# Loading and turning the FFN convolution's weights later in a one-core hybrid decoder layer

## The chip, the cores and the metric

The kernel runs on one core of a Trainium2 chip. The metric is the device time of one execution in microseconds; a median of several runs is given. A profile of one execution shows every instruction on the engines: PE (matmul) with PEld (its weight loads), DVE (vector), ACT (scalar), POOL (GpSimd), and SP, whose queue issues most of the DMAs. "L261" is line 261 of the kernel file, and names such as `raw` or `mT` are the program's tiles.

## The reference

One layer of a decoder for a prompt of 1024 tokens and 8 single-token samples, all in float32. Condition vectors `c` give shift, scale and gate of two modulations; then come a gated delta rule and sliding-window attention side by side, and an FFN with a short causal convolution on its gate. Cut to what matters here:

```python
sh1, sc1, gt1, sh2, sc2, gt2 = split(silu(c) @ w_mod + b_mod, 6)
h = rmsnorm(x, norm1_w) * (1 + sc1) + sh1
qkv, gdn_gate, beta, a, sq, sk, sv, ga, gb = split(h @ w_in)
y_a = gdn_out(delta_rule(silu(conv4(qkv, gdn_conv_w)), beta, a), gdn_gate) @ w_gdn_out
y_b = window_attention(sq, sk, sv, swa_sinks) @ w_swa_out
x = x + gt1 * ((sigmoid(ga) * y_a + sigmoid(gb) * y_b) @ w_o)
h2 = rmsnorm(x, norm2_w) * (1 + sc2) + sh2
gc = causal_dwconv3(h2 @ w_ffn_gate, ffn_conv_w) + ffn_conv_b
x = x + gt2 * ((silu(gc) * (h2 @ w_ffn_up)) @ w_ffn_down)
y = rmsnorm(x, final_norm_w)
```

`ffn_conv_w` (3 x 2816) and `ffn_conv_b` (2816) are the two inputs that the change is about. They are first needed in the FFN, in the last third of the program.

## The kernel before

Every float32 product is made of three matmuls on operands that are split into a high and a low part (`mm3`, L178 to L182; the split is L129 on ACT and L130 on DVE). Activations are kept turned, with channels on the 128 partitions, in three parts of the tokens: 384, 384 and 264 (the last with the 8 samples). Each part is normed by rows (L287 to L290: a square with a sum on ACT, a power on POOL, a scaling on DVE), turned by PE transposes (L190), modulated (L326 on ACT, L328 on DVE) and split into `b1h` and `b1l`.

The change lies in the head of the program, the first 60 us or so:

- `conditioning` (L220 on) loads `c`, applies silu and turns it into `cTr`.
- `vectors` (L192 to L218) gathers the small vectors as rows of a tile, one row for each run of 128 channels, and turns them with PE transposes, so that each becomes a column per channel tile. Biases of the modulation, the norms' weights and the delta rule's convolution are loaded on ACT's queue into `pc`. The FFN convolution's weights (66 rows of 128) and bias (22 rows) are loaded on SP's queue (L204, L205) into a tile `pp`. There are three transposes into one bank `pt`, and then copies on DVE: `vecs`, `cw`, and `fcw`, the FFN convolution's weights and bias times a half (L218).
- `modulation(lo)` makes four channel tiles of the modulation: four loads of 512 KB of `w_mod` into `qst` (L261), sixteen matmuls of 128x512 into the bank `sc` (L264), a copy `mrows` (L267), four small matmuls (L270, two instructions each in the trace), and the addition of the bias into `mT` (L271). It runs for the tiles 8, 0, 12 and 4, in this order.
- Between them stand the loads and norms of the first 384 tokens (three tiles of 128 rows: `raw`, `raw`, `V`), the modulation of channel tiles 0 to 3 as soon as the first two calls are done and of 4 to 7 after the last two, and the early weights: four loads of `w_in` (512 KB each, L135), each split into a high and a low part (`wh`/`wl`, `wmh`/`wml`, `obt`).

Who comes first on an engine is not set by the order of this code. The kernel is built with a scheduler that orders the instructions of each engine and each queue by its own estimate of when they are ready; `issue_after(x)` only forbids an instruction to stand ahead of `x`. Small edits can so move instructions far away. On each engine the instructions then run in order. DMAs report through eight semaphores that are used in turn, so that a DMA also waits for the one that had its semaphore before.

After the head, attention runs with projections of the delta rule as filler, then the delta rule's heads, the branches' output, and the second half with the FFN. `fcw` is read there (L1571 to L1575 and L1678).

## Time and profile before

| | |
|---|---|
| median of 3 runs | 2088.38 us |
| lowest and highest run | 2085.28 us, 2094.0 us |
| span of the profiled execution, first to last instruction | 2084.4 us |
| PE busy | 2012.7 us (97%) |
| DVE, ACT, POOL busy | 1347.8, 900.2, 520.2 us |
| moved by DMA | 275.75 MB |

The profile gives no device time of its own execution besides the span; the lowest of the three runs lies 0.9 us above that span and the median 4.0 us. In the rows below, a row of the timeline has the start, the duration, the engine, the line, the operation, the tiles (output<-inputs), shapes, a count and, in brackets, how long the engine had been idle before it and what ended that. "SPq" is the time in which SP's queue issues a DMA. A row of the windows has, after the stretch, the busy time and count of PE, PEld, DVE, ACT and POOL, the granted clock of PE (1.00 is full), the mean busy share of the DMA engines and the GB/s.

### The profile page before, as it was taken

How to read it: one execution, taken by the hardware profiler on the slowest of the kernel's cores; microseconds unless marked ns; L12 is line 12 of the kernel's file. 1: busy time of each engine (PE TensorE's matmuls, PEld its weight loads, DVE VectorE, ACT ScalarE, POOL GpSimd, SP SyncE). 2: the span in 40 equal slices, each digit the busy share in tenths (PEclk: the TensorE clock that was granted, in tenths of full speed). 3: DMA queues.
4: the chain of work that ended last, by engine and by line, in shares of the span. 5: the costliest groups of instructions: out<-in, count | busy, mean ns of one | idle time of the engine just before them, and what ended most of it. 6: DMA issues, size and time to landing. Idle time of an engine off the chain costs nothing.

```text
span 2084.4 us, 41297 instructions
## 1 busy us (share of the span) xinstructions
PE 2012.7 (97%) x16245; PEld 1910.2 (92%) x16245; DVE 1347.8 (65%) x2714; ACT 900.2 (43%) x2233; POOL 520.2 (25%) x594
## 2 busy tenths in 40 slices
PE   7999998999999999989989999999999999999897
PEld 4987877799999999989989999999999999999897
DVE  5755768473655647656544675578876776767756
ACT  4664545433344243432342542354444444534443
POOL 2000000121321221201111000005575466446421
PEclk9999999999999999999999999999999999999999
DMA  8256443331332322312275855323333333488862
GB/s 300 62 144 210 135 167 116 117 94 51 80 80 61 73 72 52 89 42 62 63 223 172 285 186 163 112 63 97 105 91 112 102 92 112 136 305 266 291 215 94
DMA packets 301887, 275.75 MB, mean 132 GB/s; under 512 B 59730, under 2 KB 248111, under 8 KB 301676
## 3 DMA queue, kind: packets, MB, share of 16 engines
q1 hardware_dynamic: 295642, 252.14, 39.6%
q0 software_dynamic: 5552, 20.37, 2.8%
q8 instruction: 127, 2.08, 0.4%
q14 instruction: 68, 0.56, 0.1%
q10 hardware_dynamic: 498, 0.61, 0.1%
HBM read 212.93 MB, written 62.51 MB: 132 GB/s over the span
## 4 chain that ended last, share of the span: by engine, by line
PE 83%; DVE 5%; DMA 5%; ACT 3%; issue 1%; SPq 1%; POOL 1%; DVEq 0%; POOLq 0%; ACTq 0%
PE mm L180 19%; PE mm L181 18%; PE mm L182 18%; PE wv L180 3%; PE wv L182 3%; PE wv L181 3%; PE wy L182 2%; PE wy L180 2%; PE wy L181 2%; PE pv L652 1%; PE pt L190 1%; PE tp L190 1%; DVE x L1472 1%; PE mm L264 1%; PE rc L954 1%
## 5 line engine op out<-in xcount | busy, mean ns | idle before, releaser
L180 PE MATMUL mm<-b1h,wh 128*128 128x384 f32 (+1 forms) x1520 | 496.9, 328 | 3.7 <-ACT gt L1294 1.6
L181 PE MATMUL mm<-b1l,wh 128*128 128x384 f32 (+1 forms) x1520 | 489.3, 323 | 0.0
L182 PE MATMUL mm<-b1h,wl 128*128 128x384 f32 (+1 forms) x1520 | 488.0, 323 | 0.3 <-DVE wl L130 0.3
L180 PEld LDWEIGHTS mm<-b1h,wh 128*128 128x128 f32 x1520 | 286.7, 189 | 12.4 <-issue 4.6
L181 PEld LDWEIGHTS mm<-b1l,wh 128*128 128x128 f32 x1520 | 287.1, 189 | 4.4 <-issue 3.1
L182 PEld LDWEIGHTS mm<-b1h,wl 128*128 128x128 f32 x1520 | 286.3, 189 | 3.9 <-issue 2.8
L129 ACT ACTIVATE wh<-raw 128x1024 fp32r<-128x1024 f32 x83 | 87.0, 1049 | 122.4 <-PE mm L181 70.2
L130 DVE TENSOR_TENSOR wl<-raw,wh 128x1024 fp32r<-128x1024 f32 x82 | 101.0, 1233 | 57.2 <-ACT wh L129 55.1
L181 PE MATMUL mm<-pk,w 128*128 128x260 f32 (+1 forms) x440 | 124.8, 284 | 1.1 <-DVE pk L130 1.1
L180 PE MATMUL mm<-pk,w 128*128 128x260 f32 (+1 forms) x440 | 124.8, 284 | 0.0
L182 PE MATMUL mm<-pk,w 128*128 128x260 f32 (+1 forms) x440 | 124.5, 283 | 0.0
L130 DVE TENSOR_TENSOR w<-ws,w 128x512 fp32r<-128x512 f32 x88 | 78.0, 886 | 36.9 <-ACT w L129 36.7
L1626 ACT COPY bml<-mm 128x256 f32<-128x256 f32 (+1 forms) x132 | 48.9, 371 | 100.6 <-PE mm L182 96.7
L180 PE MATMUL mm<-bmh,w 128*128 128x260 f32 (+1 forms) x320 | 90.3, 282 | 0.0
L182 PE MATMUL mm<-bmh,w 128*128 128x260 f32 (+1 forms) x320 | 90.1, 282 | 0.0
L1681 DVE SCALAR_TENSOR_TENSOR fa<-fz,fcw,fa 128x512 f32<-128x512 f32 x88 | 75.2, 874 | 18.2 <-ACT fa L1679 17.9
L180 PE MATMUL mm<-b2h,wh 128*128 128x384 f32 (+1 forms) x256 | 83.2, 328 | 2.9 <-ACT wh L129 2.8
L181 PEld LDWEIGHTS mm<-pk,w 128*128 128x128 f32 x440 | 83.2, 189 | 1.3 <-DVE pk L130 1.3
L181 PE MATMUL mm<-b2l,wh 128*128 128x384 f32 (+1 forms) x256 | 83.6, 327 | 0.4 <-DVE b2l L130 0.4
L180 PEld LDWEIGHTS mm<-pk,w 128*128 128x128 f32 x440 | 83.2, 189 | 0.2 <-ACT bml L1626 0.2
L182 PEld LDWEIGHTS mm<-pk,w 128*128 128x128 f32 x440 | 83.4, 190 | 0.0
L182 PE MATMUL mm<-b2h,wl 128*128 128x384 f32 (+1 forms) x256 | 82.8, 326 | 0.0
(645 smaller groups left out, 5886.2 us busy)
## 6 DMA issues: line engine op xcount, KB each, us to landing
raw<-in_w_in_dram SPq DMA_DIRECT2D x59, 512.0 KB
ws<-in_w_ffn_down_dram SPq DMA_DIRECT2D x55, 256.0 KB
raw<-xd SPq DMA_DIRECT2D x47, 258.0 KB
raw<-in_w_ffn_down_dram SPq DMA_DIRECT2D x47, 256.0 KB
raw<-in_w_ffn_gate_dram SPq DMA_DIRECT2D x22, 512.0 KB
raw<-in_w_ffn_up_dram SPq DMA_DIRECT2D x22, 512.0 KB
qst<-in_w_mod_dram SPq DMA_DIRECT2D x16, 512.0 KB
raw<-in_w_mod_dram SPq DMA_DIRECT2D x16, 512.0 KB
```

What stands on the lines that cost most here:

```text
L129: self.nc.scalar.activation(hi, x, AF.Copy)
L130: (eng or self.nc.vector).tensor_tensor(lo, x, hi.bitcast(F32), op=ALU.subtract)
L180: mm(ps, whi, xhi, start=first, stop=False, **kw)
L181: mm(ps, whi, xlo, start=False, stop=False, **kw)
L182: self.last_mm = mm(ps, wlo, xhi, start=False, stop=last, **kw).ins
L190: self.nc.tensor.transpose(out, in_, self.ident[:p, :p])
L264: nc.tensor.matmul(ps[32 * j:32 * j + 32], self.cT[:, k0 + j, :], ws[j // 2][:, j % 2, :], start=k0 == 0, stop=k0 > 0)
L652: nc.tensor.matmul(pv[64 * r:64 * r + 64], V[:, n - back, ch], ps[:, r::2, :], start=back == 0, stop=back == (n > 0))
L954: yield step(nc.tensor.matmul(ds, kd[:, n, :], s, start=True, stop=True))
L1472: nc.vector.scalar_tensor_tensor(x[:, :np_], ps[:, :np_], by[:, j, 8:9], x[:, :np_], op0=ALU.mult, op1=ALU.add)
L1626: self.last_copy = nc.scalar.copy(r[p, i], x[p])
L1681: nc.vector.scalar_tensor_tensor(ai[:, c:e], zi[:, j + c:j + e], col(j), ai[:, c:e], op0=ALU.mult, op1=ALU.add)
```

## The change

The two loads, the transpose and the scaling of the FFN convolution's vectors leave `vectors` and become a function of their own with two halves, `ffn_vectors`. The first half issues the loads, not ahead of the last weight load that the code has issued, into a tile `new` (a name, and a buffer, that the decays of the delta rule use later on); it is called behind the fourth early weight. The second half turns them into a bank of `pt` of its own and writes `fcw`; it is called when the first part's modulation is written.

```diff
--- before.py
+++ after.py
@@ vectors
-        rows2 = self.t(pool, [P, P], "pp")
-        nc.sync.dma_start(rows2[0:66, :], I["ffn_conv_w"][0].rearrange("j (n p) -> (j n) p", p=P))
-        nc.sync.dma_start(rows2[66:88, :], I["ffn_conv_b"][0].rearrange("(n p) -> n p", p=P))
         ps = self.t(psum, [P, 512], "pt")
         self.transpose(ps[:, 0:65], rows[0:65, 0, :])
         self.transpose(ps[:, 128:224], rows[0:96, 1, :])
-        self.transpose(ps[:, 256:344], rows2[0:88, :])
...
+    def ffn_vectors(self, pool, psum):
+
+        nc, I = self.nc, self.I
+        rows = self.t(pool, [P, P], "new", bufs=1)
+        with self.tc.issue_after(self.w_load.ins):
+            nc.sync.dma_start(rows[0:66, :], I["ffn_conv_w"][0].rearrange("j (n p) -> (j n) p", p=P))
+            nc.sync.dma_start(rows[66:88, :], I["ffn_conv_b"][0].rearrange("(n p) -> n p", p=P))
+        yield
+        ps = self.t(psum, [P, 512], "pt")
+        self.transpose(ps[:, 0:88], rows[0:88, :])
         self.fcw = self.const([P, 4, FT], "fcw")
-        nc.vector.tensor_scalar_mul(self.fcw, ps[:, 256:344].rearrange("p (j n) -> p j n", j=4), 0.5)
+        nc.vector.tensor_scalar_mul(self.fcw, ps[:, 0:88].rearrange("p (j n) -> p j n", j=4), 0.5)
+        yield
@@ run
                 self.early.append(self.win(COL_SQ + P, tags=("obt", "obt"), home=pool))
+                ffn = self.ffn_vectors(pool, psum)
+                next(ffn)
                 self.xs[2] = self.load_rows(pool, 2, ("raw", "raw", "V"))
                 self.modulate_part(pool, psum, 0, xs, self.a1, 0, range(4, KC))
+                next(ffn)
                 self.attention(pool, psum)
```

The scheduler moves much else with it. In the changed file the lines behind `vectors` are 8 higher (L280 becomes L288), those behind the new calls 11. On SP's queue, at the program's start, the rows stood so before (`raw` and `V` from `x_prompt` are the first 384 token rows):

```order
L224 DMA qst_100<-in_c_sample_dram 8x1024
L225 DMA qst_100<-in_c_prompt_dram 1x1024
L204 DMA pp_133<-in_ffn_conv_w_dram 66x128
L205 DMA pp_133<-in_ffn_conv_b_dram 22x128
L280 DMA raw_181<-in_x_prompt_dram 128x1024
L261 DMA qst_156<-in_w_mod_dram 128x2x512
L261 DMA qst_158<-in_w_mod_dram 128x2x512
L261 DMA qst_164<-in_w_mod_dram 128x2x512
L261 DMA qst_166<-in_w_mod_dram 128x2x512
L280 DMA raw_183<-in_x_prompt_dram 128x1024
L280 DMA V_185<-in_x_prompt_dram 128x1024
L261 DMA qst_204<-in_w_mod_dram 128x2x512
```

At the same place they stand so now:

```order
L232 DMA qst_100<-in_c_sample_dram 8x1024
L233 DMA qst_100<-in_c_prompt_dram 1x1024
L288 DMA raw_175<-in_x_prompt_dram 128x1024
L288 DMA raw_177<-in_x_prompt_dram 128x1024
L288 DMA V_179<-in_x_prompt_dram 128x1024
L269 DMA qst_150<-in_w_mod_dram 128x2x512
L269 DMA qst_152<-in_w_mod_dram 128x2x512
L269 DMA qst_158<-in_w_mod_dram 128x2x512
L269 DMA qst_160<-in_w_mod_dram 128x2x512
L269 DMA qst_198<-in_w_mod_dram 128x2x512
L269 DMA qst_200<-in_w_mod_dram 128x2x512
```

The two small loads are gone from here and all three token tiles stand ahead of the first `w_mod` load; the set of large loads up to the first `w_in` load, which comes two `w_mod` loads further down in both, is the same. The small loads now stand as the 29th and 30th DMA of the queue, behind the fourth `w_in` load and ahead of the third part's token rows.

On DVE, around the second modulation (`mrows`, then `mT`), the rows stood so before (`wl` is the low part of the first early weight):

```order
L267 COPY mrows_172<-sc_155 128x512
L288 TENSOR_SCALAR ss_192<-ss_192 128x1
L271 TENSOR_TENSOR mT<-sc_174,vecs 128x36
L290 TENSOR_SCALAR raw_183<-raw_183,ss_192 128x1024
L275 SCALAR_TENSOR_TENSOR a_154<-mT,vecs 128x36
L288 TENSOR_SCALAR ss_197<-ss_197 128x1
L290 TENSOR_SCALAR V_185<-V_185,ss_197 128x1024
L267 COPY mrows_220<-sc_203 128x512
L271 TENSOR_TENSOR mT<-sc_222,vecs 128x36
L328 TENSOR_SCALAR pp_232<-pt_228,a_154,mT 128x384
L130 TENSOR_TENSOR wl_289<-raw_286,wh_288 128x1024
```

They stand so now:

```order
L298 TENSOR_SCALAR V_179<-V_179,ss_191 128x1024
L275 COPY mrows_166<-sc_149 128x512
L279 TENSOR_TENSOR mT<-sc_168,vecs 128x36
L283 SCALAR_TENSOR_TENSOR a_148<-mT,vecs 128x36
L275 COPY mrows_214<-sc_197 128x512
L130 TENSOR_TENSOR wl_283<-raw_280,wh_282 128x1024
L279 TENSOR_TENSOR mT<-sc_216,vecs 128x36
L336 TENSOR_SCALAR pp_226<-pt_222,a_148,mT 128x384
```

The scaling of the second and third token tile has moved ahead of the first modulation's end, and `wl` has moved ahead of the second modulation's `mT`. The same happens at the fourth modulation, where the second weight's `wl` stands ahead of `mT`.

On PE, behind the fourth modulation, the last transposes of the first part's tokens stood before behind two matmuls of the second early weight (`mm_593`, whose first row is the transposes' neighbour here):

```order
L180 MATMUL mm_593<-b1h_10_148,wh_319 128x384
L181 MATMUL mm_593<-b1l_11_149,wh_319 128x384
L190 MATMUL pt_364<-ident,raw_181 128x128
L190 MATMUL pt_364<-ident,raw_183 128x128
L190 MATMUL pt_364<-ident,V_185 128x128
```

Now they stand behind twelve of `mm_594`, the same product, and two of the third weight (the last five of these rows and the transposes' first):

```order
L180 MATMUL mm_594<-b1h_9_142,wh_313 128x384
L181 MATMUL mm_594<-b1l_10_143,wh_313 128x384
L182 MATMUL mm_594<-b1h_9_142,wl_314 128x384
L180 MATMUL mm_623<-b1h_9_142,wmh_319 128x384
L181 MATMUL mm_623<-b1l_10_143,wmh_319 128x384
L190 MATMUL pv_369<-ident,raw_175 128x128
```

Twelve matmuls have moved from behind the transposes to ahead of them. The transpose of the FFN vectors stands about thirty matmuls further down on PE, between two transposes of the second part's tokens; on POOL a fill of `new` for the delta rule's decays, which must wait for it, now stands ahead of the third part's three powers. Further on, PE's order differs in most rows of the attention stage, in two stretches of the delta rule and in one of the output; every engine has the same operations as before.

## The prediction

> **What bounds the kernel now.** The page first: PE is busy for nearly the whole span, and the chain that ended last is 83% PE.

> ```profile
> span 2084.4 us, 41297 instructions
> PE 2012.7 (97%) x16245; PEld 1910.2 (92%) x16245; DVE 1347.8 (65%) x2714; ACT 900.2 (43%) x2233; POOL 520.2 (25%) x594
> PE 83%; DVE 5%; DMA 5%; ACT 3%; issue 1%; SPq 1%; POOL 1%; DVEq 0%; POOLq 0%; ACTq 0%
> ```

> PE is idle for 71.7 us in all (2084.4 - 2012.7), so nothing that leaves PE's work alone can win more. The change touches the head, so I read the windows there next.

> ```profile
> 5.00:10.00 5.00, 2.94 (x15) 1.51 (x15) 2.17 (x7) 1.44 (x3) 2.85 (x8) 1.00 1.02 382
> 15.00:20.00 5.00, 3.21 (x14) 1.41 (x14) 2.53 (x7) 0.86 (x2) 1.11 (x2) 0.79 1.07 378
> 20.00:25.00 5.00, 4.04 (x24) 1.69 (x22) 0.81 (x2) 1.06 (x1) 0.00 (x0) 0.87 1.09 366
> 25.00:30.00 5.00, 4.87 (x24) 2.05 (x24) 4.37 (x8) 3.22 (x6) 0.00 (x0) 1.00 1.05 387
> 45.00:50.00 5.00, 5.00 (x33) 4.90 (x32) 3.39 (x7) 4.93 (x10) 2.51 (x3) 1.00 0.41 140
> ```

> DMA is full (share over 1.0, 366 to 387 GB/s) while PE has gaps up to 25 us; from 25 us PE is nearly full, from 40 us wholly. The head is thus a race of loads against PE's first work. Third, SP's queue in the timeline, for when the loads start, and the waits of ACT and DVE, for when they land.

> ```profile
> 1.53 0.29 SPq L204 DMA_DIRECT2D pp<-in_ffn_conv_w_dram  x1
> 1.87 0.35 SPq L205 DMA_DIRECT2D pp<-in_ffn_conv_b_dram  x1
> 2.74 0.36 SPq L280 DMA_DIRECT2D raw<-in_x_prompt_dram  x1
> 3.16 2.07 SPq L261 DMA_DIRECT2D qst<-in_w_mod_dram  x4
> 5.27 0.47 SPq L280 DMA_DIRECT2D raw<-in_x_prompt_dram  x1
> ...
> 6.25 1.06 ACT L287 ACTIVATE vch<-raw 128x1024 f32<-128x1024 f32 x1 [0.96 <-DMA raw<-in_x_prompt_dram]
> 13.44 1.06 ACT L287 ACTIVATE vch<-raw 128x1024 f32<-128x1024 f32 x1 [6.04 <-DMA raw<-in_x_prompt_dram]
> 21.90 1.06 ACT L129 ACTIVATE wh<-raw 128x1024 fp32r<-128x1024 f32 x1 [6.04 <-DMA raw<-in_w_in_dram]
> 35.55 1.06 ACT L129 ACTIVATE wh<-raw 128x1024 fp32r<-128x1024 f32 x1 [6.13 <-DMA raw<-in_w_in_dram]
> ```

> These rows give one law. Large load 1 (tokens) lands at 6.25, load 6 (the second token tile) at 13.44, load 12 (the first `w_in`) at 21.90: (21.90 - 6.25)/11 = 1.42 us a load, (13.44 - 6.25)/5 = 1.44. Loads land one behind the other, at a pace that the queue's start alone shifts. Last, the steps of the modulation on DVE and PE.

> ```profile
> 15.01 0.69 DVE L267 COPY mrows<-sc 128x512 f32<-128x512 f32 x1 [4.08 <-PE sc L264]
> 17.02 0.74 DVE L290 TENSOR_SCALAR raw<-raw,ss 128x1024 f32<-128x1024 f32 x1
> 20.88 2.11 PE L264 MATMUL sc<-qst,cTr 128*32 128x512 f32 x12
> 23.04 0.69 DVE L267 COPY mrows<-sc 128x512 f32<-128x512 f32 x1 [3.69 <-PE sc L264]
> 24.88 0.20 DVE L271 TENSOR_TENSOR mT<-sc,vecs 128x36 f32<-128x36 f32 x1 [1.15 <-PE sc L270]
> 25.13 1.05 PE L264 MATMUL sc<-qst,cTr 128*32 128x512 f32 x4 [0.29 <-DVE mT L271]
> 25.70 1.22 DVE L130 TENSOR_TENSOR wl<-raw,wh 128x1024 fp32r<-128x1024 f32 x1
> 34.31 1.92 PE L264 MATMUL sc<-qst,cTr 128*32 128x512 f32 x16 [0.29 <-DVE mT L271]
> 38.15 0.20 DVE L271 TENSOR_TENSOR mT<-sc,vecs 128x36 f32<-128x36 f32 x1 [1.15 <-PE sc L270]
> 39.12 0.44 PE L190 MATMUL pt<-ident,raw 128*128 128x128 f32 x2 [0.55 <-DVE pp L328]
> ```

> The second modulation is late although its loads are not: load 11, its last, should land at 6.25 + 10 x 1.42 = 20.5, yet PE does twelve of its matmuls in one run at 20.88 to 22.99, behind the transposes of token tiles that landed as loads 6 and 7 and were scaled from 17.02 on.

> **Part by part.** *The two loads leave the queue's head.* Token load 1 stands where the first of them stood: it is issued at 1.53 instead of 2.74, 1.21 us earlier. It has no wait for an earlier DMA now, and the third token tile is the one that waits. Every load of equal rank lands 1.21 us earlier; the 44 KB less are 0.1 us more, left out. [...]

> *Token tiles 2 and 3 move ahead of the first modulation's loads.* Load 7 is now the first modulation's last: 6.25 - 1.21 + 6 x 1.42 = 13.6. With its last four matmuls (1.05) that modulation ends near 14.7, no later than before, when its copy began at 15.01; and the norms' scalings now fall into that wait. Load 11 is still the second modulation's last: 5.04 + 14.2 = 19.2, and its last four matmuls (1.05) end near 20.3 instead of 22.99.

> *`wl` moves ahead of `mT` on DVE.* That takes some back: the first `w_in` (load 12) lands at 21.90 - 1.21 = 20.69, ACT's high part takes 1.06, DVE's low part 1.22, so `mT` comes at about 22.97 and not at 21.8. Queued behind `wl` on DVE are `mT` and the first modulated tile, and PE's third modulation waits for them. Before `mT` was at 24.88: 1.9 us gained.

> *To the fourth modulation* PE runs the same instructions without a gap (25.13 to 34.31), so the 1.9 us hold; its last load, number 20, is due at 5.04 + 19 x 1.42 = 32.0, in time. Its `mT` waits for the second `wl`: `w_in` at 35.55 - 1.21 = 34.34, plus 1.06 and 1.22, 36.6 against 38.15: 1.5 us. But PE no longer waits there. Before, it did two matmuls and stood still for 0.55 us until the transposes; now twelve more stand ahead of them. Two later rows give their pace:

> ```profile
> 40.50 0.34 PE L182 MATMUL mm<-b1h,wl 128*128 128x384 f32 x1
> 40.68 0.33 PE L180 MATMUL mm<-b1h,wh 128*128 128x384 f32 x1
> ```

> Twelve at 0.175 to 0.18 us are 2.1 us. By the steps above the transposes would end near 39.8, as they do before, with these twelve done: the head is 2.1 us ahead. I take **-2.1**, with bounds of 0 (a later wait eats it) and -3.2 (22.99 - 20.3, and the 0.55, if `wl` takes nothing back).

> *The moved operations themselves.* One transpose and one scaling:

> ```profile
> 8.37 0.35 PE L190 MATMUL pt<-ident,pp 88*128 88x88 f32 x1
> 9.07 0.24 DVE L218 TENSOR_SCALAR fcw<-pt 128x88 f32<-128x88 f32 x1
> ```

> At 8 us PE was waiting anyway; at 45 us it is full (5.00 of 5), so the transpose now costs 0.1 to 0.35. I take 0.2, the middle. Its loads go behind the fourth `w_in`, which waits for the second `wl` (36.6), and PE is there thirty matmuls behind 39.8, near 45: they have some 8 us, and if that cover were gone, PE and POOL's powers behind the fill of `new` would wait for one load, 1.4 us. DVE has 3.39 of 5 busy there, so the scaling is taken at 0, at most 0.24. The sum: -2.1 + 0.2 = **-1.9**.

> *The reshuffle behind the head.* No operation is added, but PE's order changes in the attention stage. Its gaps lie here:

> ```profile
> 340.00:350.00 10.00, 9.12 (x93) 7.63 (x91) 8.88 (x15) 4.87 (x10) 1.01 (x1) 1.00 0.44 148
> 350.00:360.00 10.00, 6.16 (x66) 4.65 (x64) 7.96 (x33) 7.98 (x37) 0.00 (x0) 1.00 0.13 52
> 360.00:370.00 10.00, 7.95 (x52) 5.68 (x52) 7.11 (x25) 6.46 (x25) 0.51 (x1) 1.00 0.10 23
> 370.00:380.00 10.00, 7.63 (x49) 5.44 (x49) 5.96 (x21) 6.09 (x27) 0.00 (x0) 1.00 0.14 55
> ```

> PE idles 0.88 + 3.84 + 2.05 + 2.37 = 9.1 us, waiting for the softmax between short runs of filler. The new order there has the same pattern (mostly six filler matmuls between the score groups, one place with none), so I take 0; the bounds are a gain of 9.1 and as much lost.

> **Sum.** The span goes from 2084.4 to 2082.5. The runs lie up to 9.6 us above the span and their median 4.0; I carry 1.9 us over to the median: 2088.38 - 1.9 = 2086.5 us. About 0.5%, 10.4 us, is what a measurement of this kernel can tell from no change (its own three runs spread over 8.7), so this counts as no change.

> **The rivals.**

> *The head's gain is eaten.* Attention's first scores wait for the softmax on DVE and ACT, and ACT is full at 45 us (4.93 of 5). If those set the pace, PE's lead of 2.1 us becomes a wait: 2088.4. For it speaks ACT's row; against it PE's, which is as full.

> *Slower: filler misplaced in attention.* Each score group there lacks cover by about a microsecond now. If the new order puts filler where PE has cover and leaves it out where it hasn't, six matmuls (1.05 us) of stall are added at each such place; to pass 10.4 us it would take twelve places, the 9.1 us more than doubled: 2086.5 + 12.6 = 2099. I see one place of this kind in the new order, which speaks against it.

> *Faster: filler covers attention.* The reverse, all 9.1 us filled and the head's 1.9: 2077.4, just past 0.5%. The same pattern speaks against it.

> *A colder PE.* The granted clock was 0.79 in the window of 15 to 20 us, where PE was busy for 3.21 of 5. With tokens ahead of `w_mod`, PE waits for the first modulation's loads until about 9 us and again between them. If that lowers the clock for as long again as in the two windows from 15 to 25 us, 5 x 0.21 + 5 x 0.13 = 1.7 us are lost and the gain is nearly gone: 2088.2. [...]

> **How the numbers follow.** The forecast (head ahead by about 2 us, the rest within 3) has 0.62; the eaten gain 0.18 and the colder PE 0.08, both no change; slower by attention 0.06; faster by attention 0.06. So 0.06 faster, 0.88 the same, 0.06 slower. The range takes the two cases of no gain, a few microseconds of reshuffle either way and the spread of a median of such runs (about 3 us): 2080 to 2094.

> **What would show it.** Right: the first token load issued near 1.5; the second modulation's copy near 20.3 and its `mT` near 23; `wl` before it; no gap of PE before the transposes at 39 us; PE's sum over the first 60 us up by about 2 us; idle between 340 and 380 us within 3 of 9.1. Wrong: loads that land at the old times, DVE waiting for `w_in` ahead of `mT` for longer than 1.2 us, PE waiting at the FFN vectors' transpose, or any stage behind 100 us that changes by more than the head.

## The result and the profile after

The changed kernel takes 2092.61 us (median of 21 runs, 2088.42 to 2101.8) against 2088.28 us for the kernel before in 21 runs beside them: ratio 1.0023, 95% interval [1.0012, 1.0034]. That is within 0.5%, as forecast, but slower by 4 to 5 us where 1.9 us were to be gained. The profiled execution has a span of 2088.8 us (before 2084.4). First its page: PE is busy 2.0 us longer with as many instructions, and its idle time has grown by 2.4 us (2088.8 - 2014.7 = 74.1 against 71.7).

```profile
span 2088.8 us, 41308 instructions
PE 2014.7 (96%) x16245; PEld 1911.1 (91%) x16245; DVE 1355.7 (65%) x2714; ACT 902.1 (43%) x2233; POOL 525.4 (25%) x594
```

**The head.** SP's queue (first rows) starts with the tokens, as forecast; ACT has the first `w_in`, and DVE the modulations' steps.

```profile
1.53 0.83 SPq L288 DMA_DIRECT2D raw<-in_x_prompt_dram  x2
2.77 0.33 SPq L288 DMA_DIRECT2D V<-in_x_prompt_dram  x1
```

```profile
21.04 1.06 ACT L129 ACTIVATE wh<-raw 128x1024 fp32r<-128x1024 f32 x1 [11.43 <-DMA raw<-in_w_in_dram]
```

```profile
16.54 0.69 DVE L275 COPY mrows<-sc 128x512 f32<-128x512 f32 x1 [4.13 <-PE sc L272]
...
20.72 0.69 DVE L275 COPY mrows<-sc 128x512 f32<-128x512 f32 x1 [1.84 <-PE sc L272]
22.13 1.23 DVE L130 TENSOR_TENSOR wl<-raw,wh 128x1024 fp32r<-128x1024 f32 x1 [0.72 <-ACT wh L129]
23.27 0.19 DVE L279 TENSOR_TENSOR mT<-sc,vecs 128x36 f32<-128x36 f32 x1
...
35.38 0.69 DVE L275 COPY mrows<-sc 128x512 f32<-128x512 f32 x1 [1.82 <-PE sc L272]
```

The second modulation's copy starts at 20.72 (before 23.04; 20.3 forecast) and its `mT` at 23.27 (before 24.88). But the fourth is only 0.9 us ahead (PE's last matmul of it ends at 35.31, before at 36.24). The windows show what took the rest: the granted clock.

```profile
25.00:30.00 5.00, 5.00 (x20) 2.37 (x19) 2.52 (x5) 1.85 (x4) 0.00 (x0) 0.68 1.06 388
...
35.00:40.00 5.00, 4.19 (x23) 3.56 (x20) 3.99 (x6) 4.06 (x7) 0.01 (x1) 0.84 0.90 321
40.00:45.00 5.00, 5.00 (x27) 4.91 (x27) 3.82 (x9) 4.66 (x10) 2.06 (x3) 0.82 0.60 204
```

Cut finer, the 0.68 turns out to be one stretch of 3.41 us at exactly 0.50, between stretches at 1.00:

```profile
21.36:24.78 3.42, 2.32 (x17) 1.28 (x17) 2.08 (x5) 1.99 (x4) 0.00 (x0) 1.00 1.05 386
24.78:28.19 3.41, 3.41 (x13) 1.62 (x11) 2.74 (x5) 2.07 (x4) 0.00 (x0) 0.50 1.05 386
28.19:31.60 3.41, 3.41 (x20) 2.19 (x19) 0.69 (x1) 0.00 (x0) 0.00 (x0) 1.00 1.06 374
```

In the stretch ahead of it PE waited for `mrows` and `mT` and did the eight small matmuls of 128x9 between. A full PE at half clock for 3.41 us does 1.7 us less work, an estimate (0.50 x 3.41). A second such stretch stands at 38.43 us. Over the first 60 us PE is busy for 46.71 us, before for 46.63, so the 2 us more that were to show are not there. Ahead of the end, this profile has 13 such stretches; the first profile of the kernel before has 10. One of these stands at 17.90 us: the 0.79 and 0.87 that the prediction read there come from one stretch at exactly 0.50 as well, seen through windows of 5 us.

**Attention.** Idle is 0.32 + 2.70 + 0.40 + 2.53 = 5.95 us between 340 and 380 us (before 9.1), 3.2 us less, but at a clock of 0.79 and 0.87 in two of the windows, 10 x 0.21 + 10 x 0.13 = 3.4 us:

```profile
340.00:350.00 10.00, 9.68 (x71) 7.91 (x70) 7.89 (x16) 6.50 (x18) 1.23 (x1) 1.00 0.35 118
350.00:360.00 10.00, 7.30 (x88) 5.49 (x86) 8.27 (x33) 7.54 (x34) 0.00 (x0) 0.79 0.19 77
360.00:370.00 10.00, 9.60 (x59) 6.59 (x57) 7.35 (x23) 6.08 (x25) 0.51 (x1) 0.87 0.10 23
370.00:380.00 10.00, 7.47 (x49) 4.79 (x48) 6.93 (x22) 5.56 (x23) 0.00 (x0) 1.00 0.15 56
```

**The delta rule.** Set side by side by tiles, the traces are 0.7 us apart at 845 us (half of the `rc<-S,K` steps) and 5.5 us apart three quarters through them, at 1012.7 before and 1018.2 after. PE's waits of over 0.25 us from 845 to 1024 us sum to 7.35 us before and 11.01 after. The largest differences stand where one head's scan (its serial chain of steps `rc<-S,K`, `rc<-y,W`, `rc<-s,kd`) ends and the inverse for the next head needs the tile `W`; this place is called the junction below. PE before, without the projections (`mm`, matmuls that depend on none of this and serve as filler):

```profile
1004.57 0.38 PE L954 MATMUL rc<-s,kd 128*128 128x128 f32 x2
...
1006.32 1.14 PE L1074 MATMUL tp<-W,UZ 64*64 64x64 f32 x16
...
1008.37 0.66 PE L190 MATMUL tp<-ident,K 128*128 128x128 f32 x4 [0.33 <-ACT W L1075]
1009.77 0.66 PE L190 MATMUL rc<-ident,vn 128*128 128x128 f32 x4 [0.74 <-DVE vn L976]
```

and after:

```profile
1007.40 0.38 PE L962 MATMUL rc<-s,kd 128*128 128x128 f32 x2
...
1009.13 1.14 PE L1082 MATMUL tp<-W,UZ 64*64 64x64 f32 x16 [1.13 <-ACT W L1073]
...
1011.47 1.11 PE L190 MATMUL tp<-ident,K 128*128 128x128 f32 x4 [0.61 <-ACT W L1083]
1014.43 1.12 PE L190 MATMUL rc<-ident,vn 128*128 128x128 f32 x4 [1.84 <-DVE vn L984]
```

The waits are 1.13 + 0.61 + 1.84 = 3.58 us instead of 0.33 + 0.74 = 1.07, and the clock falls behind them for two stretches:

```profile
1007.82:1011.23 3.41, 1.91 (x22) 1.43 (x20) 1.38 (x2) 3.27 (x10) 0.29 (x1) 1.00 0.06 19
1011.23:1014.64 3.41, 1.33 (x5) 0.93 (x6) 1.48 (x5) 2.73 (x16) 1.02 (x1) 0.50 0.53 154
1014.64:1018.06 3.42, 3.42 (x17) 3.42 (x17) 1.97 (x4) 2.48 (x13) 0.00 (x0) 0.50 0.28 113
```

The order of PE tells why (rows of the program's order, cut). Before, the scan's last reading of `W` (`rc<-y,W`) stood 34 rows ahead of `tp<-W,UZ`, and its last step ten projections ahead of it:

```
L950 MATMUL rc_1702_10747<-y_1700_10743,W_741_4535 128x128
...
L954 MATMUL rc_1704_10751<-s_1703_10749,kd_1562_9872 128x128
L958 MATMUL o_1681_10700<-s_1703_10749,A_1574_9924 128x128
L182 MATMUL mm_1789_11351<-b1h2_14_152,wl_1784_11292 128x264
...
L182 MATMUL mm_1789_11351<-b1h2_14_152,wl_1784_11292 128x264
L1074 MATMUL tp_1771_11185<-W_741_4535,UZ_1745_10993 64x64 x8
```

Now it stands 13 rows ahead, and the ten projections stand ahead of the last step:

```
L958 MATMUL rc_1703_10748<-y_1701_10744,W_742_4536 128x128
L182 MATMUL mm_1790_11352<-b1h2_13_146,wl_1785_11293 128x264
...
L182 MATMUL mm_1790_11352<-b1h2_13_146,wl_1785_11293 128x264
L962 MATMUL rc_1705_10752<-s_1704_10750,kd_1563_9873 128x128
L966 MATMUL o_1682_10701<-s_1704_10750,A_1575_9925 128x128
L1082 MATMUL tp_1772_11186<-W_742_4536,UZ_1746_10994 64x64 x8
```

`W` has one buffer. The copies that fill it for the next head (ACT) may start only when `rc<-y,W` is done, and stand behind `s`, which needs the same step:

```profile
1006.39 0.37 ACT L960 ACTIVATE s<-rc,c 128x128 f32<-128x128 f32 x1 [1.42 <-PE rc L958]
1006.65 1.67 ACT L1057 COPY W<-T 32x256 f32<-32x256 f32 x4
1008.35 0.73 ACT L1073 COPY W<-tp 32x256 f32<-32x256 f32 x2
```

Before, they ran five microseconds earlier, under PE's projections:

```profile
1001.28 1.67 ACT L1049 COPY W<-T 32x256 f32<-32x256 f32 x4
1002.97 0.74 ACT L1065 COPY W<-tp 32x256 f32<-32x256 f32 x2
```

The change edits none of these instructions.

### The profile page after: what moved, and what is told of

It reads as the page before. It is cut to its first block, busy times and chain, and to the rows that moved or that the text cites. A ratio compares the mean times of both kernels' runs of the same rounds, so it can differ in the third digit from the quotient of the medians.

```text
span 2088.8 us, 41308 instructions
## 1 busy us (share of the span) xinstructions
PE 2014.7 (96%) x16245; PEld 1911.1 (91%) x16245; DVE 1355.7 (65%) x2714; ACT 902.1 (43%) x2233; POOL 525.4 (25%) x594
## 4 chain that ended last, share of the span: by engine, by line
PE 75%; DMA 9%; DVE 8%; ACT 3%; SPq 1%; issue 1%; POOL 1%; DVEq 0%; POOLq 0%; ACTq 0%
PE mm L180 17%; PE mm L182 17%; PE mm L181 17%; PE wv L180 2%; PE wv L182 2%; PE wv L181 2%; DMA ws<-in_w_ffn_down_dram 2%; PE pv L660 1%; PE wy L180 1%; PE wy L181 1%; PE wy L182 1%; DVE pk L130 1%; PE pt L190 1%; DMA raw<-in_w_ffn_down_dram 1%; PE mm L272 1%
## 5 line engine op out<-in xcount | busy, mean ns | idle before, releaser
L180 PE MATMUL mm<-b1h,wh 128*128 128x384 f32 (+1 forms) x1520 | 498.7, 330 | 6.1 <-ACT gt L1302 3.1
L182 PE MATMUL mm<-b1h,wl 128*128 128x384 f32 (+1 forms) x1520 | 489.9, 324 | 0.3 <-DVE wl L130 0.3
L180 PEld LDWEIGHTS mm<-b1h,wh 128*128 128x128 f32 x1520 | 286.9, 189 | 15.6 <-issue 4.6
L182 PEld LDWEIGHTS mm<-b1h,wl 128*128 128x128 f32 x1520 | 286.6, 189 | 5.3 <-issue 3.6
L129 ACT ACTIVATE wh<-raw 128x1024 fp32r<-128x1024 f32 x83 | 87.0, 1048 | 132.1 <-PE mm L181 73.5
L130 DVE TENSOR_TENSOR wl<-raw,wh 128x1024 fp32r<-128x1024 f32 x82 | 101.1, 1234 | 60.9 <-ACT wh L129 57.5
L180 PE MATMUL mm<-pk,w 128*128 128x260 f32 (+1 forms) x440 | 124.5, 283 | 0.0
L182 PE MATMUL mm<-pk,w 128*128 128x260 f32 (+1 forms) x440 | 124.2, 283 | 0.0
L130 DVE TENSOR_TENSOR w<-ws,w 128x512 fp32r<-128x512 f32 x88 | 77.7, 884 | 36.8 <-ACT w L129 36.7
L182 PE MATMUL mm<-bmh,w 128*128 128x260 f32 (+1 forms) x320 | 90.6, 283 | 0.0
L180 PE MATMUL mm<-bmh,w 128*128 128x260 f32 (+1 forms) x320 | 90.3, 282 | 0.0
L1689 DVE SCALAR_TENSOR_TENSOR fa<-fz,fcw,fa 128x512 f32<-128x512 f32 x88 | 73.7, 857 | 18.4 <-ACT fa L1687 18.1
L180 PE MATMUL mm<-b2h,wh 128*128 128x384 f32 (+1 forms) x256 | 82.6, 325 | 1.9 <-ACT wh L129 1.9
L180 PEld LDWEIGHTS mm<-pk,w 128*128 128x128 f32 x440 | 83.0, 189 | 0.2 <-ACT bml L1634 0.2
L182 PEld LDWEIGHTS mm<-pk,w 128*128 128x128 f32 x440 | 83.1, 189 | 0.0
L182 PE MATMUL mm<-b2h,wl 128*128 128x384 f32 (+1 forms) x256 | 82.3, 324 | 0.0
```

The lines of the kernel that those rows point to most:

```text
L129: self.nc.scalar.activation(hi, x, AF.Copy)
L130: (eng or self.nc.vector).tensor_tensor(lo, x, hi.bitcast(F32), op=ALU.subtract)
L180: mm(ps, whi, xhi, start=first, stop=False, **kw)
L182: self.last_mm = mm(ps, wlo, xhi, start=False, stop=last, **kw).ins
L1689: nc.vector.scalar_tensor_tensor(ai[:, c:e], zi[:, j + c:j + e], col(j), ai[:, c:e], op0=ALU.mult, op1=ALU.add)
```

## Experiments

Theories: **order** (the scheduler's new order of the delta rule costs what is lost), **late work** (the loads, the late transpose, the scaling or the later fill of `new` cost it), **clock** (the head makes PE run at half clock more often). In many kernels the order of every engine is written out, so that one part of it can be changed and nothing else moves (the diff is cut; `NoSync` ties the order and adds no wait):

```diff
     Step(ctx, tc, I, O).run()
+    for k in ORDER:
+        i = by[k]
+        if i.engine in last:
+            tc.add_manual_dep(i, last[i.engine].name, _D(_C.NoSync, _R.DATA), reason="order")
+        last[i.engine] = i
```

`ORDER` is made of the orders of before and after; the diffs below say in words of which. Each was timed in 5 to 12 runs beside the kernel before on the same chip, but for the first two, which are one profiled execution each. The last column is the time lost to the clock, (1 - mean granted clock) x span, as a mean over a kernel's runs with its standard error, and for the kernel before on the same chip. "Warm" stands for matmuls without use in the waits of the early modulations.

| run | ratio to before, 95% interval | lost to the clock, us: this / before |
|---|---|---|
| the change | 1.0023 [1.0012, 1.0034] | 26.1 ± 1.2 / not recorded |
| e3 late turn only | 1.0005 [0.9992, 1.0017] | 20.7 ± 0.7 / 20.4 ± 0.9 |
| e4 ACT's queue | 1.0039 [1.0025, 1.0054] | 23.3 ± 1.0 / 20.4 ± 0.9 |
| e5 delta put back | 1.0015 [1.0002, 1.0028] | 23.1 ± 1.0 / 20.1 ± 0.6 |
| e6 delta alone | 1.0026 [1.0015, 1.0037] | 24.2 ± 1.4 / 20.1 ± 0.6 |
| e7 `mT` first | 1.0005 [0.9995, 1.0015] | 22.0 ± 1.2 / 20.1 ± 0.6 |
| e8 warm head | 1.0060 [1.0046, 1.0074] | 20.2 ± 0.5 / 20.1 ± 0.6 |
| e9 head and attention alone | 1.0003 [0.9990, 1.0015] | 22.8 ± 1.3 / 21.6 ± 0.7 |
| e10 change, warm | 1.0018 [1.0006, 1.0029] | 23.2 ± 0.8 / 21.6 ± 0.7 |
| e11 before, warm | 0.9986 [0.9975, 0.9998] | 18.1 ± 0.6 / 21.6 ± 0.7 |
| e12 parts together | 0.9995 [0.9982, 1.0008] | 20.2 ± 0.6 / 21.6 ± 0.7 |
| e13 junction back | 1.0016 [1.0005, 1.0027] | 23.6 ± 1.6 / 22.8 ± 0.5 |
| e14 junction alone | 1.0015 [1.0004, 1.0026] | 23.0 ± 1.1 / 22.8 ± 0.5 |
| e15 change, old order | 1.0005 [0.9996, 1.0014] | 23.1 ± 1.0 / 22.8 ± 0.5 |
| e16 old order, warm | 0.9998 [0.9989, 1.0006] | 20.1 ± 0.6 / 22.8 ± 0.5 |
| e17 old order mended | 1.0001 [0.9987, 1.0016] | 22.2 ± 1.2 / 20.9 ± 0.8 |
| e18 mended, warm | 0.9994 [0.9982, 1.0006] | 18.8 ± 0.9 / 20.9 ± 0.8 |

**What is fixed and what varies.** Both kernels again, without an edit.

> The kernel before, unchanged, profiled a second time, to see what of the profile is fixed. Theory of the order (the loss is PE idle time that the new order makes in the second half of the delta rule, 845 to 1018 us): the gaps of PE there sum to 7.4 us again within 1, at the same places. Theory of the clock (the loss is stretches at half clock that come by chance): the number of such stretches ahead of the end differs from the 10 of the first profile by two or more, and the span moves by about 1.7 us for each.

> The changed kernel, unchanged, profiled a second time. Theory of the order: the gaps of PE from 845 to 1018 us sum to 10.7 us again within 1, with those of 1.1 to 1.8 us near 975, 1008 and 1012 us. Theory of the clock: the stretches at half clock stand at other places than in the first profile, and their number differs from 13 by two or more; if they are then as few as the 10 of before, the span comes down to 2084.

PE's waits from 845 to 1024 us repeat: 7.64 us (7.35) and 11.01 (11.01), those at the junction as 1.13, 0.61 and 1.98. The half clock stands in part at other places: 12 stretches instead of 10 before, 16 instead of 13 after; at the junction the change again has two, before none. Between 340 and 380 us PE idles 9.1 us again before, and 7.0 after. Stage by stage, the steps `rc<-S,K` serve as marks. To the half of them the change takes 845.7 and 847.6 us in its two profiles, before 845.0 and 845.6; from there to the last of them 272.7 and 272.4, before 268.2 and 268.0; from there to the end 970.4 and 969.7, before 971.2 and 970.9. So the delta rule alone holds 4.4 to 4.5 us, about the whole difference of the spans (4.4 and 5.1). In the head the change's gain was gone this time, its second modulation ended at 22.94 us and not at 20.62, behind a stretch at half clock from 19.7. So the ends in a single profile can't tell a gain of 2 us in this head from none.

**Is it the late work?** The loads stay at the queue's head, transpose and scaling come late:

```diff
+                ffn = self.ffn_vectors(pool, psum)
+                next(ffn)
                 self.vectors(pool, psum)
...
                 self.early.append(self.win(COL_SQ + P, tags=("obt", "obt"), home=pool))
-                ffn = self.ffn_vectors(pool, psum)
-                next(ffn)
```

> The loads stay at the head of SP's queue; only the transpose and the scaling come late, as in the change. PE's order differs from the kernel before in ten rows of the head and nowhere else. Theory of the order: as the kernel before, ratio 1.0000 within 0.0006 (the late transpose, 0.2 us, is all). Theory of the late work itself (transpose, scaling and the tile's later fill cost what is lost): slower by 4 us or more, ratio 1.002 as in the change. Theory of the clock: as before within the spread of its runs.

1.0005, and the interval excludes 4 us (1.0019): late turning is not the cause. The reverse, tokens first and nothing late:

```diff
-        nc.sync.dma_start(rows2[0:66, :], I["ffn_conv_w"][0].rearrange("j (n p) -> (j n) p", p=P))
+        nc.scalar.dma_start(rows2[0:66, :], I["ffn_conv_w"][0].rearrange("j (n p) -> (j n) p", p=P))
```

(and the bias likewise).

> The two loads go to ACT's queue and are turned early as before, so SP's queue starts with the tokens as in the change, and nothing comes late. PE's order is new in the head and in attention, but in the second half of the delta rule it stands near that of before (94 rows differ; 609 in the change). Theory of the order: the head's 2.1 to 2.4 us are won and not lost again in the delta rule, ratio 0.9990 (2086 us), PE's gaps from 845 to 1018 us near 7.4 us. Theory that attention eats the head's gain: ratio 1.000. Theory of the late work itself: also 0.999. Theory of the clock (tokens first make PE cold at other places in the head, by about two stretches of 1.7 us): ratio 1.0005 to 1.001, with stretches at half clock between 24 and 40 us as in the change.

All expectations missed: 1.0039. The waits in the delta rule are near those of before (8.4 us from 845 to 1024 us), but the order is a third one, with three stretches at half clock at 19.9 us, 4.1 us more waits from 60 to 300 us (6.45 against 2.32), and a last quarter of the `rc<-S,K` steps of 104.7 us instead of 100.5. Leaving the queue's head is thus no gain by itself when the scheduler answers with a new order.

**Is it the delta rule's order?** One stretch of the order is exchanged in each direction; within it, the two orders differ from 925 to 1064 us.

```diff
-ORDER = after
+ORDER = after to 845 us, before to 1115 us, after to the end
```

> The changed kernel, with the order of every engine written out: as in the change up to the middle of the delta rule (845 us) and behind its end (1115 us), but between them as in the kernel before. Theory of the order (4.4 to 4.8 us of the loss arise from that stretch's new order): ratio to before 1.0023 - 0.0022 = 1.0001; PE's gaps there fall from 11.0 to about 7.5 us, and the half clock behind 1011 us is gone. Rival (that stretch only shows what is late from elsewhere, the head or a transfer): ratio stays 1.0023.

```diff
-ORDER = before
+ORDER = before to 845 us, after to 1115 us, before to the end
```

> The kernel before (loads at the queue's head, early transpose), with the order of every engine written out: only from 845 to 1115 us it is that of the change. Theory of the order: 4.4 to 4.8 us slower than before, ratio 1.0022, with gaps of 11 us and half clock near 1011 us. Rival (the stretch is late because of the head): ratio 1.000.

Alone, on the kernel before, the stretch costs 0.26% [0.15, 0.37], as much as the whole change. Put back in the change it gave less than expected, 1.0015 and not 1.0001, which these runs hardly tell from the change's 1.0023; the waits fell to 7.45 us. Its profile, which is its slowest run, took 975.0 us behind the last `rc<-S,K` step, where the change's own profiles took 970.4 and 969.7 in the same order; e10's, again in that order, took 974.9. So part of what is left there varies from run to run and need not lie in the delta rule. In each of the five profiles with the change's junction (both of the change, e6, e10, e14) PE falls to half clock there, for one stretch or two; in the fifteen with the old one it never does.

**Is it one junction?** The same exchange for the junction alone. On PE the exchanged rows run from 965 to 1008 us of the two traces, on ACT and DVE to 1021, so the stretch starts earlier than the expectations say.

```diff
-ORDER = after
+ORDER = after to the junction, before through it, after to the end
```

> The changed kernel with the order of every engine written out; it is that of the kernel before in one stretch alone, about 981 to 1021 us, where a head of the delta rule ends and the next one's inverse waits for its last step. Theory of the junction (there the last step of the scan stands behind ten projection matmuls that used to stand behind it, so nothing covers the waits for W and vn, 1.13, 0.61 and 1.84 us, and PE falls to half clock for 6.8 us): 2.0 us of gaps and 1.7 to 3.4 us of half clock go, ratio 1.0023 - 0.0018 to 0.0026, that is 0.9997 to 1.0005. Rival (the loss is spread over the delta rule and the head): ratio 1.0018 or more.

```diff
-ORDER = before
+ORDER = before to the junction, after through it, before to the end
```

> The kernel before with the change's order in that one stretch alone. Theory of the junction: 3.7 to 5.4 us slower than before, ratio 1.0018 to 1.0026. Rival (spread): ratio 1.0005 or less.

Alone it costs 0.15% [0.04, 0.26], 3.1 us, and its profile has the waits and both stretches of the change:

```profile
1009.76 1.14 PE L1074 MATMUL tp<-W,UZ 64*64 64x64 f32 x16 [1.13 <-ACT W L1065]
...
1012.10 1.08 PE L190 MATMUL tp<-ident,K 128*128 128x128 f32 x4 [0.61 <-ACT W L1075]
1015.06 1.11 PE L190 MATMUL rc<-ident,vn 128*128 128x128 f32 x4 [1.88 <-DVE vn L976]
```

```profile
1008.80:1012.21 3.41, 1.84 (x21) 1.54 (x22) 1.23 (x1) 3.29 (x11) 0.29 (x1) 0.99 0.06 19
1012.21:1015.63 3.42, 1.54 (x7) 1.14 (x8) 1.62 (x4) 2.71 (x17) 1.02 (x1) 0.50 0.52 153
1015.63:1019.04 3.41, 3.41 (x18) 3.40 (x17) 1.64 (x3) 2.46 (x13) 0.00 (x0) 0.51 0.39 155
```

Over its runs, though, the time lost to the clock is that of before (23.0 ± 1.1 against 22.8 ± 0.5), so on the mean the half clock at the junction is not shown to cost anything there; the waits from 965 to 1020 us, 4.2 us instead of 1.6, make up most of the 3.1. For the whole stretch (e6) the clock takes 24.2 ± 1.4 against 20.1 ± 0.6.

Put back, the junction won only 0.07%, which these runs can't tell from nothing. At the seam of the two orders a wait stands that neither kernel has, and the waits of the stage still sum to 10.45 us:

```profile
968.71 0.66 PE L190 MATMUL rc<-ident,vn 128*128 128x128 f32 x4 [1.38 <-DVE vn L984]
```

So by the run that adds it the junction carries 0.15 of the 0.23%, with an interval from a sixth to all of it; the run that takes it away does not confirm this, and is probably spoilt by its seam.

**Head and attention.** The change's order up to 845 us, then that of before.

```diff
-ORDER = after
+ORDER = after to 845 us, before to the end
```

> The changed kernel with the order of every engine written out: as in the change up to 845 us (head and attention), from there to the end as in the kernel before. PE's gaps up to the end of attention are 2.7 us fewer than before in both. Forecast of the prediction for this part: 1.9 to 2.7 us faster, ratio 0.9989. Theory of the clock: the head has two stretches at half clock where PE is full, before has one where it waits, and attention about one more, so what the gaps give is lost again: ratio 1.000 within 0.001, and the time lost to the clock per run is 2 to 4 us above that of before (20.2 us).

1.0003: the forecast for this part (0.9991) lies at the interval's edge. Five runs look at the half clock in the head. First DVE's order, on top of the delta rule put back:

```diff
-ORDER = ... mrows, wl, mT, pp ... mrows, wl, mT, pp
+ORDER = ... mrows, mT, pp, wl ... mrows, mT, wl, pp
```

> As the kernel with the delta stage put back, and on DVE the second and the fourth modulation's mT stand ahead of the early weights' low parts (wl) again. Theory of the clock in the head (a stretch of about 2 to 3 us in which PE does next to nothing at a modulation's end makes the next 3.4 us run at half clock, which costs 1.7 us): the wait ahead of the third modulation falls from 0.99 to 0.3 us, and half clock behind it comes less often; 0.7 to 2.4 us better than with the delta stage put back alone, ratio 0.999 to 0.9998. Rival (the wait for wl only moves to PE's first projections): the same ratio as with the delta stage put back alone, 1.0001.

Then matmuls without use, nine in each of the four modulations (the diff is simplified; they stand right beside the small matmuls in the written-out order):

```diff
+        full = self.t(psum, [P, 512], ptag)
+        for _ in range(5):
+            nc.tensor.matmul(full[:, 64:320], self.ident, self.cT.rearrange("p k c -> p (k c)"), start=True, stop=True)
         for i in range(4):
             nc.tensor.matmul(ps[:, i, :], rows[:, i * P:(i + 1) * P], self.strips, start=True, stop=True)
+        for _ in range(4):
+            nc.tensor.matmul(full[:, 64:320], self.ident, self.cT.rearrange("p k c -> p (k c)"), start=True, stop=True)
```

> As the kernel with the delta stage put back, and PE does nine matmuls of 128x256 without use around each of the four early modulations' small matmuls (five while it waits for mrows, four while it waits for mT; about 1.2 us in each modulation, of which some 0.3 lie beyond the waits). Theory of the clock in the head: no stretch at half clock between 15 and 45 us in the profile, where the changed kernel had two in both of its profiles; the head ends 3.4 us earlier less 1 us of added work, ratio 0.999. Rival (the half clock comes from something else than PE standing still): the stretches stay, and the head is 1 us later, ratio 1.0006.

`mT` first: 1.0005 against 1.0015, the way expected but within the intervals. The warm head has no half clock from 15 to 45 us, yet comes to 1.0060 (its base, e5, to 1.0015): its bank is that of `sc`, so the matmuls wait for `mrows` themselves, and one of 128x256 takes two instructions of 0.24 us on the mean:

```profile
17.97 2.43 PE L281 MATMUL sc<-cTr,ident 128*128 128x256 f32 x10 [0.85 <-DVE mrows L276]
```

With a bank of their own and only two of them, they fit the wait for `mrows`. This was put on the change, on before, and on the parts that looked best (again simplified):

```diff
+self.bank = self.t(self.pool("warm", 1, PSUM, ctx=c), [P, 512], "warm")
...
+        for _ in range(2):
+            nc.tensor.matmul(self.bank[:, 0:256], self.ident, self.cT.rearrange("p k c -> p (k c)"), start=True, stop=True)
         for i in range(4):
```

> The changed kernel, its order written out as it is, with two matmuls of 128x256 without use, into a bank of their own, on PE ahead of each of the four early modulations' small matmuls, where PE waits 0.8 to 0.9 us for mrows (they take about 1 us, 0.1 to 0.2 more than the wait, in sum 0.5 us). Theory of the clock in the head: one or two stretches at half clock between 15 and 45 us go; the time lost to the clock falls from 26.1 to 23 to 24.5 us a run, ratio to before 1.0010 to 1.0018. Rival (the half clock does not come from PE standing still): they stay, ratio 1.0023 to 1.0026.

> The kernel before, its order written out as it is, with the same matmuls without use in the same four waits. Theory of the clock: the one stretch near 17.5 us goes or not, which is worth little because PE waits there anyway; ratio 0.9993 to 1.0003. Rival (matmuls without use cost their whole time, 4 us): ratio 1.002.

In the third of them the order is mixed as well:

```diff
-ORDER = after
+ORDER = after to 845 us, with mT ahead of wl as above, before to the end
```

> The parts that looked best together: the change's order up to 845 us with mT ahead of wl on DVE, the order of before from there, and the matmuls without use in the four waits. Theory of the clock and the order: gaps 2.7 us fewer than before up to attention's end, none of the two stretches at half clock in the head, nothing lost in the delta rule; ratio 0.9985 to 0.9993. Rival (the delta rule and the end give the gain back whatever is in the head): ratio 1.000 or above.

On the change they moved 1.0023 to 1.0018, on the best parts they gave 0.9995 where 0.9985 to 0.9993 was expected; neither is told from no gain. The kernel before with these eight matmuls is the only version that is faster than before: 0.9986, 2084.63 us against 2087.75, and better than its own expectation. Its interval ends at 0.9998, so among this many versions it could be chance; the time lost to the clock, 18.1 ± 0.6 against 21.6 ± 0.7 us, speaks against that. Its windows have the full clock in the whole head, where before had 0.79 and 0.87:

```profile
15.00:20.00 5.00, 3.89 (x23) 1.45 (x22) 1.93 (x6) 1.15 (x2) 1.11 (x2) 1.00 1.07 376
20.00:25.00 5.00, 4.31 (x24) 2.19 (x23) 2.14 (x4) 2.27 (x4) 0.00 (x0) 1.00 1.09 364
```

Over all profiles: with before's order in the head, 12 stretches at half clock between 15 and 45 us in 7 profiles; with the change's, 9 in 6; with matmuls in the waits, 1 in 6 (in e10, behind a wait of 1.31 us for `mT` that they don't cover); e4, with its own order, has 3. So the half clock comes with these waits. That the change's head has more of it is not borne out; of its 9, though, 7 stand behind 24 us, where PE is full, and of before's 12 only 5, too few to tell. The theory of the clock is right on where the half clock comes from, but with e9 at 1.0003 the head's clock is not the cause of the loss.

**The change without a new order.** Loads and late transpose as in the change, all else as before:

```diff
-ORDER = after
+ORDER = before, with the two loads, their transpose, fcw and the fill of new where after has them
```

> The change itself without the new order: the loads behind the fourth early weight, the late transpose and scaling, the later fill of new on POOL, and everything else on every engine in the order of the kernel before. Theory of the order (what loses is the order alone): all loads land 1.2 us earlier, ratio 0.9994 to 1.0000. Rival (the loads or the late transpose cost by themselves): ratio 1.001 or more.

The second has the two matmuls of the diff above as well.

> The same with the two matmuls without use in each of the four waits of the early modulations. Theory of the clock and the order: the loads' 1.2 us and the head's half clock (1.4 times 1.7 us, as the kernel before won by these matmuls) add up: ratio 0.9980 to 0.9990, better than before and than the change. Rival (the gains hide each other): as the kernel before with these matmuls, 0.9986, or worse.

1.0005 and 0.9998, but PE waits in both where neither kernel does: the next transposes need the bank `pt`, which `fcw` has to read first, and `fcw` stands on DVE behind `obt`.

```profile
47.25 0.24 PE L190 MATMUL pt<-ident,new 88*128 88x88 f32 x1
50.27 0.33 PE L190 MATMUL pt<-ident,qst 128*128 128x128 f32 x1 [2.78 <-DVE fcw L225]
```

```profile
48.84 1.21 DVE L130 TENSOR_TENSOR obt<-raw,obt 128x1024 fp32r<-128x1024 f32 x1
49.98 0.24 DVE L225 TENSOR_SCALAR fcw<-pt 128x88 f32<-128x88 f32 x1
```

With `fcw` three rows further up:

```diff
-ORDER = ... ss, qst, ss, obt, fcw
+ORDER = ... ss, fcw, qst, ss, obt
```

> The change in the order of the kernel before, as in the run before the last, but the scaling fcw stands three rows further up on DVE, ahead of the last second-part scaling and the fourth weight's low part, for which it had made PE wait 2.78 us at the bank pt. Theory (the change itself is a small gain, hidden there by that wait): the wait falls to 1.2 us or less, as in the kernel before, ratio 0.9990 to 0.9998. Rival (the change gains nothing even so): 1.0000 or more.

> The same with the two matmuls without use in each of the four waits of the early modulations. Theory: the loads' gain and the head at full clock add up, ratio 0.9975 to 0.9988, the best version. Rival: no better than the kernel before with these matmuls, 0.9986 or more.

The wait is 0.34 us, the ratio 1.0001 [0.9987, 1.0016]: no gain that these runs can tell from none, nor a loss. With the matmuls it is 0.9994, no better than before with them. So the moved loads, transpose and scaling show no loss in the old order (1.0005 and 1.0001), and the new order of the delta rule alone shows the whole of it (1.0026); the intervals of the first two still touch the lower end of the change's.

## Why the prediction was wrong

**The reshuffle behind the head is the step that failed.** It priced attention alone ("so I take 0", bounds 9.1 us either way). The reorder of the delta rule, visible in the changed kernel's order, had no term and no rival, and so was put at nothing without a reason; the only slower rival sat in attention. Alone it costs 5.4 us (0.26%), at the junction 3.1 us. The wait was foreseeable in kind: `W` has one buffer, and the projections that covered its refill stood on the other side of the scan's last step. The sign to look for was written down ("any stage behind 100 us that changes by more than the head") and is what the profile shows.

**The loads' lead** held: tokens issued at 1.53, the first `w_in` there at 21.04 (20.69 worked out), and in the first profile the second modulation's copy 2.3 us earlier, `wl` ahead of `mT`, `mT` at 23.27 (22.97 worked out). **The first modulation** was not "no later than before": its copy moved from 15.01 to 16.54. The loads did not hold it; PE ran without a gap from 10.69 to 16.45 us, and each 128x512 matmul that began before 14.4 us took 1.06 us, where the later ones at full clock take 0.59 to 0.65. The second modulation's sixteen matmuls had to wait for the first's `mT` (18.45), so they ended at 20.62 and not at 20.3:

```profile
11.10 1.92 PE L272 MATMUL sc<-qst,cTr 128*32 128x512 f32 x4
...
15.38 1.06 PE L272 MATMUL sc<-qst,cTr 128*32 128x512 f32 x8
...
18.70 1.92 PE L272 MATMUL sc<-qst,cTr 128*32 128x512 f32 x16 [0.29 <-DVE mT L279]
```

**The head's -2.1** does not show as time: the head and attention alone measure 1.0003, with an interval [0.9990, 1.0015] that barely reaches it. The sign for it, 2 us more of PE's work in the first 60 us, failed: 46.71 us against 46.63. The waits up to attention's end are 2.9 us fewer in the first profile, but nearly all of that stands in attention; in the first 60 us they sum to 13.3 us against 13.4 (12.3 against 13.2 in the second pair). Besides, the forecast left out that one half-clock stretch more or less, 1.7 us, moves the head by nearly as much from run to run. The rival of a colder PE had its price right, the 1.7 us of one stretch, and the head as its place; that the change brings more of them is not borne out, 9 in 6 profiles against 12 in 7.

**The late transpose** (0.2) is consistent with e3, but "so the scaling is taken at 0, at most 0.24" is a weak step: in e15 the same scaling made PE wait 2.78 us, because it stood behind one long instruction in DVE's queue (`obt`, 1.21 us).

**Attention** came out near 0, as taken, but by luck: in that profile 3.2 us fewer waits stand against 3.4 us at half clock.

The range held the time because it allowed for a few microseconds of reshuffle; the likeliest case had the wrong sign, so this speaks for the width of the range and not for the mechanism. Still open: e5 and e9 differ only in the order behind 1115 us, and their ratios (1.0015 and 1.0003) overlap, so what that part costs is not settled (the two pairs of profiles show no loss there); nor is the sum, since the change's runs lost 26.1 us to the clock on a chip where before's clock was not recorded.

## What to carry to other kernels

When a scheduler orders the program, compare the order of every stage and price the places where filler changes sides with a serial chain, above all at the refill of a tile with one buffer; the edited lines may be the smallest part of the change. Waits that lie close together can bring half clock with them: at the junction they left PE busy for 1.91 of 3.41 us in the changed kernel's first profile, and the next 6.83 us had a clock of 0.50; over the runs of e14, which has the same junction, the half clock was not shown to cost time (23.0 ± 1.1 against 22.8 ± 0.5 us lost). A few matmuls without use in a wait of known length, in a bank of their own, gave 0.14% [0.02, 0.25] on the kernel before, and on the other versions no gain that could be told from none; the earlier loads showed no gain in any order.

## What the runs showed of the hardware

```profile
1007.77:1011.18 3.41, 2.34 (x17) 1.56 (x15) 3.19 (x4) 3.19 (x17) 0.71 (x1) 1.00 0.23 61
1011.18:1014.59 3.41, 2.88 (x23) 2.60 (x22) 1.37 (x4) 3.19 (x19) 0.00 (x0) 1.00 0.73 251
```

- Ahead of the clock's first record (14.49 and 14.54 us) the windows of these two profiles show 1.00, yet the 128x512 matmuls that began from 8.66 to 13.37 us in before and from 11.10 to 13.58 us in after took 1.06 us, as those at half clock did (18.40 us in before, 26.55 us in after); behind it, those of the head that stand wholly at full clock took 0.59 to 0.62 us.
- A float32 matmul of 128x256 with 128x128 weights takes two instructions of 0.24 us each on the mean (e8, 2.43 us for ten). Those of 128x512 with 128x32 weights are one instruction each, and where sixteen stood together (34.31 us, before) four started within 0.02 us of one another and the next four 0.43 to 0.45 us later, 1.92 us for all.
